# A two-block fp32 network on one core: tanh for sigmoid, powers on GpSimd for square roots, opened output products, regrouped layer A, and a scheduler that counts shared-port time

## Chip, core and metric

The kernel runs on one NeuronCore of a Trainium2 chip. The metric is the device time of one execution in microseconds (us). All inputs and outputs are fp32.

## The reference, cut to what matters

The program is one forward pass over 512 tokens of width 1024: a gated linear recurrence (layer A), sliding-window attention (layer B), a second block with windowed attention and grid attention, and an MLP. Every norm is a root mean square over the width.

```python
# layer A, R = 1536, in blocks of 96 for the two gates
u = rmsnorm(x) @ w_in; xb, gate = u[:R], u[R:]
xb = conv4(xb)
r, i = sigmoid(xb @ wr + br), sigmoid(xb @ wi + bi)
a = exp(-8 r softplus(-lam)); b = sqrt(1 - a*a) * (i * xb)
x = x + (scan(a, b) * silu(gate)) @ w_out
# keys and values of layer B from this x; layer B, 16 heads of 64, window 128, sinks
q, gate = split(rmsnorm(x) @ w_in); q = rmsnorm(q per head)
x = x + (attention(q, k, v, sinks) * silu(gate)) @ w_out
# block 2: windowed attention a, grid attention b, merged by sigmoid gates
q_a, k_a, v_a, q_b, k_b, v_b, g_a, g_b = split(rms_norm(x) @ w_in)
m = sigmoid(g_a + bg_a) * (y_a @ w_pa) + sigmoid(g_b + bg_b) * (y_b @ w_pb)
x = x + m @ w_out
x = x + square(relu(rms_norm(x) @ w_up)) @ w_down
return rms_norm(x)
```

## The kernel before

The activations stand transposed: 128 features on the partitions, 512 tokens along a row. Each fp32 product is made from three products of rounded halves: a value is split in a high half (a copy to type fp32r, helper `A` with `AF.Copy`, line 305, 309 or 314) and a low half (value minus high half, `TT`, line 329, or `STT`, line 343, on VectorE). `mm3` issues high·high, high·low and low·high, all 512 columns wide, through `MMS` (line 370). Weights are split in the same way, per piece of 1024 columns: `raw_task` loads a piece by DMA (line 400) into a slot of the pool FB, `hi_task` lets ScalarE, VectorE (first eight pieces) or GpSimd make the high half, and `lo_task` always has VectorE make the low half. FB has 38 slots of 512 columns and holds nearly every intermediate; PSUM has 8 banks.

Jobs are Python generators that yield operations. The class `Sched` runs them all, gives every operation a booked duration, and in each step emits the one that can start first and scores best; so the order on every engine is a plan, and on the chip each engine works through its own list in that order. An operation may have options on several engines, and then the one that is booked to end first is taken. The function `main` runs the TensorE jobs strictly in the order in which `add` and `then` list them.

- `gemm` makes one 128-feature output: for 8 k pieces it is 24 matmuls, and its results are taken from PSUM by an `evac` task. `gemm_open(w, ns, kcut, ...)` first runs the k pieces below `kcut` for all outputs of `ns`, and then the rest, so that TensorE has work on the early activations while the later ones are being made.
- Layer A (`layer_a`): 12 products `xb` (convolution, split, restacking by DMA), four jobs `rg_job` (30 matmuls each, for both gates of three feature groups), 12 products `ga` for the output gate. `rg_post` makes tanh, exp, square root and the scan (line 817) for the three; `ga_evac` waits for each third product and then does sigmoid, two products and the split of `y_a`. `a_w_out` opens three outputs over the first 9 of 12 pieces.
- Norms (`rstd_chain`): the sum of squares goes through a matmul with ones, ScalarE's square root, and VectorE's reciprocal (line 363) over 512 columns; only norm b goes by tokens, that is over 4 columns, and then back by a diagonal matrix and a second matmul with ones.
- Layer B (`layer_b`): `w_kv`, then 16 products `b_w_in` with the 16 attention units (`attn_unit`, four heads by one block of 128 tokens each) spread between them. A unit makes the masks (`PMUL`, line 357, GpSimd), score matmuls (256 wide), maxima (line 959, VectorE), exponentials (ScalarE), a division (GpSimd), transposes (line 394), and the products with v (256 wide). `q1_scale` makes the norms of q: square root on ScalarE, reciprocal and products on VectorE. `b_w_out` opens four outputs over 6 of 8 pieces; piece k needs `y1[k]`, which is whole when all four units of its group are.
- Block 2 (`block2`), the same in kind; its end is `w_pb` (opened), whose results `pb_evac` turns into `mrg`, and then `w_out_2`, 8 plain products over `mrg`. `mlp` follows, and `fin_stats`, `fin_task` and `fin_out` make the last norm and store it.

Sigmoid, square root and exp stand in three different tables of ScalarE (tanh stands with exp, and with sigmoid as well); `Sched` books a switch at 1283 ns and avoids it by a score.

Of the kernel before, what the change touches and what calls it, by code (L numbers as in the profile page):

```python
# [89 lines left out]
class Sched:  # L90
# [43 lines left out]
    def run(self):  # L134
        while self.tasks:
# [97 lines left out]
def kernel(ctx: ExitStack, tc: tile.TileContext, io: dict, out: bass.AP):  # L233
# [592 lines left out]
    def ga_evac(n, b):  # L826
        j = n - KR
        gat[j] = yield from scaled(b, n_a)
        if j % 3 == 2:
            sg = {}  # L830
            for i in range(j - 2, j + 1):
                sg[i] = yield from fa.get()
                yield A(f_(sg[i]), f_(gat[i]), AF.Sigmoid)
            for i in range(j - 2, j + 1):
                yield TT(f_(gat[i]), f_(gat[i]), f_(sg[i]), ALU.mult)
                fa.free(sg[i])
            for i in range(j - 2, j + 1):
                yield lambda: i in hs
# [1008 lines left out]
```

## Time and profile before

| | us |
|---|---|
| median of three runs | 1162.11 (1161.6 to 1163.76) |
| the profiled execution, device time | 1162.27 |
| its span, first to last instruction | 1160.4 |
| TensorE busy in it | 1129.6 (97%) |
| VectorE, ScalarE, GpSimd busy | 772.6, 419.4, 273.9 |

Busy time counts an engine as busy while one of its instructions is under way. The mean granted clock of TensorE over the span is 0.988 of 2.4 GHz. A table by stretches gives for each engine the busy time and, in brackets, the number of instructions; matmuls overlap, so their mean duration is longer than the distance from one to the next, and the rate is read from the chain of waits, which gives a length and a count.

### The profile page before, as it was taken

The page shows a single profiled execution, that of the slowest core. Times are in us where ns is not written, and L with a number is a line of the kernel's source. Part 1 is how long each engine was busy: PE and PEld are TensorE (multiplying, and loading weights), DVE is VectorE, ACT ScalarE, POOL GpSimd, SP SyncE. Part 2 cuts the span into 40 slices and gives each one's busy share as a digit, 9 for nine tenths or more (in the row PEclk, how much of TensorE's full clock was granted, in tenths as well). Part 3 has the DMA queues.
Part 4 walks back from the last instruction along what each step waited for, and adds up shares of the span by engine and source line. Part 5 has one row for each costly group of instructions (what it writes and reads, how often), then busy time and mean ns, then how long its engine had stood idle before and what let it go on. Part 6 is the DMA issues. An engine that isn't in the chain of part 4 may idle for free.

```text
span 1160.4 us, 14950 instructions
## 1 busy us (share of the span) xinstructions
PE 1129.6 (97%) x5444; PEld 943.4 (81%) x5444; DVE 772.6 (67%) x1362; ACT 419.4 (36%) x809; POOL 273.9 (24%) x356
## 2 busy tenths in 40 slices
PE   8999799999999899999999999899999999999997
PEld 5888588888888678888888888688888888888887
DVE  8999998756778888567666464867654224556332
ACT  5348841224887641166542225111111121111111
POOL 2111152023644633033223223312110002112000
PEclk9999899999999899999999999999999999999999
DMA  7252436207242330821371643432243322233001
GB/s 284 76 140 58 132 122 209 91 1 206 68 123 87 101 127 1 239 89 64 91 236 57 175 134 116 142 130 91 73 127 91 122 78 91 73 109 109 1 1 73
DMA packets 45641, 125.85 MB, mean 108 GB/s; under 512 B 6144, under 2 KB 8576, under 8 KB 45568
## 3 DMA queue, kind: packets, MB, share of 16 engines
q1 hardware_dynamic: 45568, 124.90, 34.3%
q8 instruction: 43, 0.70, 0.2%
q14 instruction: 30, 0.25, 0.1%
HBM read 104.95 MB, written 2.10 MB: 92 GB/s over the span
## 4 chain that ended last, share of the span: by engine, by line
PE 90%; DVE 6%; ACT 1%; DMA 1%; issue 1%; SPq 0%; DVEq 0%; ACTq 0%
PE ps L370 87%; PE ps L394 3%; DVE fb L329 2%; DVE rb L329 2%; DVE fb L817 1%; ACT rb L305 1%; DVE fb L959 0%; DMA rb<-rb 0%; DMA fb<-in_x 0%; ACT fb L305 0%; SPq L400 0%; DMA fb<-in_wg 0%; DVE fb L343 0%; DVE rb L309 0%; ACT L305 0%
## 5 line engine op out<-in xcount | busy, mean ns | idle before, releaser
L370 PE MATMUL ps<-rb 128*128 128x512 f32 (+2 forms) x5008 | 1095.5, 378 | 18.3 <-ACT rb L305 10.3
L370 PEld LDWEIGHTS ps<-rb 128*128 128x128 f32 x5008 | 895.0, 189 | 193.9 <-ACT rb L305 12.5
L329 DVE TENSOR_TENSOR rb<-fb,rb 128x1024 fp32r<-128x1024 f32 (+5 forms) x301 | 298.7, 1015 | 62.4 <-ACT rb L305 57.0
L314 POOL TENSOR_SCALAR rb<-fb 128x1024 fp32r<-128x1024 f32 (+5 forms) x154 | 173.7, 1137 | 677.9 <-PE ps L370 541.4
L305 ACT ACTIVATE rb<-fb 128x512 fp32r<-128x512 f32 (+5 forms) x127 | 94.6, 752 | 335.4 <-DVE fb L343 154.0
L329 DVE TENSOR_TENSOR fb<-ps,fb 128x512 f32<-128x512 f32 (+2 forms) x170 | 102.4, 604 | 154.8 <-PE ps L370 141.5
L329 DVE TENSOR_TENSOR fb<-fb 128x512 f32<-128x512 f32 (+1 forms) x140 | 99.8, 725 | 25.2 <-ACT rb L305 20.9
L357 POOL TENSOR_SCALAR fb<-fb,sm 128x256 f32<-128x256 f32 (+2 forms) x128 | 68.7, 556 | 152.0 <-DVE sm L363 105.3
L329 DVE TENSOR_TENSOR rb<-ps,rb 128x512 fp32r<-128x512 f32 (+1 forms) x92 | 58.1, 640 | 42.1 <-ACT rb L305 39.8
L305 ACT ACTIVATE rb<-ps 128x512 fp32r<-128x512 f32 (+1 forms) x92 | 50.5, 558 | 89.0 <-PE ps L394 66.4
L305 ACT ACTIVATE fb<-fb,sm 128x256 f32<-128x256 f32 (+2 forms) x128 | 65.3, 512 | 36.4 <-DVE sm L351 25.9
L305 ACT ACTIVATE rb<-fb,vec 128x512 fp32r<-128x512 f32 x41 | 28.5, 720 | 111.2 <-DVE fb L329 109.2
L343 DVE SCALAR_TENSOR_TENSOR fb<-ps,fb 128x512 f32<-128x512 f32 x36 | 24.9, 691 | 52.5 <-PE ps L370 52.4
L305 ACT ACT_TABLE_LOAD x44 | 56.5, 1283 | 7.9 <-DVE fb L736 4.3
L305 ACT ACTIVATE fb<-fb 128x512 f32<-128x512 f32 (+1 forms) x60 | 35.1, 610 | 62.6 <-DVE fb L329 60.8
L394 PE MATMUL ps<-ident,fb 128*128 128x128 f32 x328 | 48.3, 273 | 3.4 <-POOL fb L357 1.9
L394 PEld LDWEIGHTS ps<-ident,fb 128*128 128x128 f32 x328 | 39.2, 140 | 10.5 <-POOL fb L357 2.3
L305 ACT ACTIVATE fb<-ps 64x256 f32<-64x256 f32 (+1 forms) x57 | 23.6, 414 | 44.1 <-PE ps L370 34.5
L959 DVE CUSTOM_DVE_ANT_0 fb<-ps,fb 128x256 f32<-128x256 f32 (+1 forms) x64 | 28.5, 486 | 12.5 <-DMA fb<-in_mbe 5.2
L357 POOL TENSOR_SCALAR fb<-fb,sm_qs 128x256 f32<-128x256 f32 (+1 forms) x64 | 31.1, 509 | 10.5 <-DMA fb<-in_mk 10.5
L343 DVE SCALAR_TENSOR_TENSOR rb<-fb,vec,rb 128x512 fp32r<-128x512 f32 x41 | 31.3, 781 | 0.3 <-ACT rb L305 0.2
L959 DVE CUSTOM_DVE_ANT_0 fb<-ps,fb,sm_qt 128x256 f32<-128x256 f32 (+1 forms) x64 | 26.4, 440 | 4.8 <-PE ps L370 3.5
(71 smaller groups left out, 286.9 us busy)
## 6 DMA issues: line engine op xcount, KB each, us to landing
fb<-in_w_in SPq DMA_DIRECT2D x34, 512.0 KB, 3.8
rb<-rb SPq DMA_DIRECT2D x128, 128.0 KB, 3.0
fb<-in_w_up SPq DMA_DIRECT2D x32, 512.0 KB, 3.5
fb<-in_w_down SPq DMA_DIRECT2D x32, 512.0 KB, 3.6
fb<-in_a_w_in SPq DMA_DIRECT2D x22, 512.0 KB, 4.5
fb<-in_b_w_in SPq DMA_DIRECT2D x16, 512.0 KB, 4.5
fb<-in_a_w_out SPq DMA_DIRECT2D x8, 512.0 KB, 3.6
fb<-in_w_out SPq DMA_DIRECT2D x8, 512.0 KB, 3.7
```

The costliest lines, as they stand in the source:

```text
L305: opts = [("ACT", dur, lambda: nc.scalar.activation(out=o, in_=i, func=fn, **kw), TABLES.get(fn))]
L314: lambda: nc.gpsimd.tensor_scalar(out=o, in0=i, scalar1=1.0, scalar2=1.0, op0=ALU.mult, op1=ALU.mult), None,
L329: lambda: nc.vector.tensor_tensor(out=o, in0=a, in1=b, op=op), None,
L343: lambda: nc.vector.scalar_tensor_tensor(out=o, in0=a, scalar=s, in1=b, op0=op0, op1=op1), None,
L357: lambda: nc.gpsimd.tensor_scalar(out=o, in0=a, scalar1=s, scalar2=1.0, op0=ALU.mult, op1=ALU.mult), None,
L370: nc.tensor.matmul(out=o, lhsT=l, rhs=r, start=st, stop=sp)
L394: nc.tensor.transpose(o, i, ident)
L817: nc.vector.tensor_tensor_scan(out=f_(h), data0=f_(rg[0, j]), data1=f_(th[j]), initial=0.0, op0=ALU.mult, op1=ALU.add)
L959: nc.vector.tensor_tensor_reduce(out=pt[:, h, 0:nk], in0=PS[:, b, o0:o0 + nk], in1=m, scale=sc, scalar=-3.0e38, op0=ALU.add, op1=ALU.max, ...
```

## The change

1. Sigmoid becomes tanh of half the argument: `ga_evac`, `g1_evac` and `g2_evac` work on each product alone; the factors 0.5 and the `+1` go into products that were there (`STT` for `TT`). The gates r and i of layer A keep their sigmoid, and `rg_post` its square root.
2. Square roots with a reciprocal become a power of -0.5 on GpSimd (`GTT`, booked 350 ns + 165 ns a column). All norms go by tokens (4 columns), `q1_scale` does both halves at once on GpSimd (16 columns, five small operations behind each other), and the last norm uses it too (2 columns).
3. `layer_a` alternates its groups; `a_w_out` opens four outputs over 8 pieces. `w_kv`, the first three of `w_in_2`, the first three of `w_out_2` and of `w_up` are opened over 4 pieces; their first pieces of weights are half as wide.
4. `Sched` lengthens a VectorE or GpSimd operation that has no PSUM input by a share of its overlap with the other, and GpSimd is charged 600 ns more where another engine could do the work.

```diff
+AVOID = 600.0
+STRETCH = {"DVE": 0.3, "POOL": 0.6}
...
+    def _shared(self, eng, op, s, dur):
+        if any(k[0].startswith("ps") for k in op.r):
+            return dur
+        mine, other = (("DVE", "POOL"), ("POOL", "DVE"))[eng == "POOL"]
+        ov = sum(max(0.0, min(s + dur, e) - max(s, b)) for b, e in self.port[other])
+        self.clock[other] += ov * STRETCH[other]
+        dur += ov * STRETCH[mine]
...
-                        if best is None or s + o[1] < best[0]:
+                        f = s + o[1] + (AVOID if o[0] == "POOL" and len(t.op.opts) > 1 else 0.0)
+                        if best is None or f < best[0]:
...
+    def GTS(o, a, s1, s2):
+        return Op([("POOL", 420.0, ...
+    def GTT(o, a, b, op):
+        return Op([("POOL", 350.0 + 165.0 * _free(o) if op == ALU.pow else 200.0, ...
...
     def rstd_chain(nrm):
-        if not nrm.tokens:
-            yield MMS([(p_(b), ones, acc, True, True, 858.0)])
-            yield A(f_(bc), p_(b), AF.Sqrt, scale=1.0 / D, bias=eps)
-            yield RECIP(f_(bc), f_(bc))
...
-        yield A(std, PS[:, b, 0:4], AF.Sqrt, scale=1.0 / D, bias=eps)
-        yield RECIP(col, std)
+        yield TS(ms, PS[:, b, 0:4], 1.0 / D, ALU.mult, EPS, ALU.add)
+        yield GTT(col, ms, half[:, 0:4], ALU.pow)
...
     def ga_evac(n, b):
+        gat[j] = yield from scaled(b, n_a, 0.5)
+        yield A(f_(sg), f_(gat[j]), AF.Tanh)
+        yield STT(f_(gat[j]), f_(sg), 1.0, f_(gat[j]), ALU.add, ALU.mult)
+        yield lambda: j in hs
+        yield TT(f_(hs[j]), f_(hs[j]), f_(gat[j]), ALU.mult)
...
     def layer_a():
-        xb(2, 9)
+        xb(2, 6)
+        ga(0,1)
         rg_job(0)
+        xb(6, 9)
+        ga(1, 3)
+        rg_job(1)
         xb(9, 12)
-        rg_job(1)
-        ga(0, 2)
+        ga(3, 5)
         rg_job(2)
-        ga(2, 4)
+        ga(5, 7)
         rg_job(3)
-        ga(4, 12)
+        ga(7, 12)
-        gemm_open("a_w_out", [0, 1, 2], 9, KR, y_a, ev, 1)
+        gemm_open("a_w_out", [0, 1, 2, 3], 8, KR, y_a, ev, 1)
...
     def q1_scale(hg):
+        yield TT(v(t), v(PS[:, b, 0:16]), bc(c2), ALU.mult)
+        yield GTS(t, t, 1.0 / 64, EPS)
+        yield GTT(sd, t, half, ALU.pow)
+        yield GTT(t, t, sd, ALU.mult)
+        yield GTT(v(sd), v(sd), bc(n_b.col), ALU.mult)
+        yield GTT(v(t), v(t), bc(n_b.std), ALU.mult)
...
+        gemm_open("w_kv", [0, 1], 4, KD, act_kv, lambda n, b: (v1_evac if n else k1_evac)(n, b), 1)
+        gemm_open("w_in_2", list(first), 4, KD, act_m, lambda n, b: first[n](n, b), 1)
+        gemm_open("w_out_2", [0, 1, 2], 4, KD, mrg, ev, 1)
+        gemm_open("w_up", [0, 1, 2], 4, KD, act_f, up_evac)
...
     def fin_stats(th):
-            yield A(stdf[:, k:k + 1], PS[:, bs[k], 0:1], AF.Sqrt, scale=1.0 / D, bias=eps)
+            yield TS(stdf[:, k:k + 1], PS[:, bs[k], 0:1], 1.0 / D, ALU.mult, EPS, ALU.add)
-        yield RECIP(colf[:, c], stdf[:, c])
+        yield GTT(colf[:, c], stdf[:, c], half[:, 0:2], ALU.pow)
```

The plan changes on every engine. Three places follow, each as the engine's list reads before and in the changed kernel.

VectorE at the norm of layer A, before: the low halves of two weight pieces, the reciprocal, then the first products taken from PSUM.

```order
L329 TENSOR_TENSOR fb<-fb 128x512 x2
L329 TENSOR_TENSOR rb<-fb,rb 128x1024 x2
L363 RECIPROCAL fb<-fb 128x512
L343 SCALAR_TENSOR_TENSOR lt<-vec 128x12
L736 MEMSET fb 128x3 x4
L329 TENSOR_TENSOR rb<-fb,rb 128x1024
L329 TENSOR_TENSOR fb<-ps,fb 128x512 x4
```

VectorE at the same place, changed:

```order
L346 TENSOR_TENSOR fb<-fb 128x512 x2
L346 TENSOR_TENSOR rb<-fb,rb 128x1024 x2
L368 TENSOR_SCALAR sm<-ps 128x4
L346 TENSOR_TENSOR fb<-ident,col_a 128x512
L759 MEMSET fb 128x3 x3
L346 TENSOR_TENSOR fb<-ps,fb 128x512 x2
```

The reciprocal over 512 columns is gone; a 4-column step and the diagonal stand in its place, with the power on GpSimd between them.

ScalarE in the middle of layer B, before (`sm_qs` are the norms of q, `fb,sm<-fb,sm` the exponentials with their sums):

```order
L305 ACTIVATE fb,sm<-fb,sm 128x256 x4
L305 ACTIVATE sm<-sm 128x4
L305 ACT_TABLE_LOAD
L305 ACTIVATE sm_qs_0_2373<-sm_qt_0_2372,eps 128x8
L305 ACT_TABLE_LOAD
L305 ACTIVATE fb,sm<-fb,sm 128x256 x2
L305 ACTIVATE rb<-ps 128x512
```

ScalarE there, changed:

```order
L322 ACT_TABLE_LOAD
L322 ACTIVATE fb,sm<-fb,sm 128x128 x4
L322 ACTIVATE sm<-sm 128x4
L322 ACTIVATE fb,sm<-fb,sm 128x256 x2
L322 ACTIVATE rb<-fb 128x1024
L322 ACTIVATE fb,sm<-fb,sm 128x256 x3
L322 ACTIVATE sm<-sm 128x4
L322 ACTIVATE fb,sm<-fb,sm 128x256 x3
```

The load shown last is the last one of the whole list: 45 loads become 18, of which 16 are at the start and in layer A in the changed kernel and 15 before.

TensorE at the end of `b_w_in`, before; the first row holds its last three matmuls, the 512-wide ones behind it are `b_w_out`, the 256-wide ones scores or products with v, and `ident` marks transposes:

```order
L370 MATMUL ps<-rb 128x512 x6
L370 MATMUL ps<-rb 128x256 x22
L370 MATMUL ps<-rb 128x512 x3
L370 MATMUL ps<-rb 128x256 x8
L394 MATMUL ps<-ident,fb 128x128 x4
L370 MATMUL ps<-rb 128x512 x6
L394 MATMUL ps<-ident,fb 128x128 x8
L370 MATMUL ps<-rb 128x256 x8
L394 MATMUL ps<-ident,fb 128x128 x4
L370 MATMUL ps<-rb 128x256 x16
```

TensorE there, changed; again the first row holds the last three of `b_w_in`:

```order
L396 MATMUL ps<-rb 128x512 x15
L420 MATMUL ps<-ident,fb 128x128 x4
L396 MATMUL ps<-rb 128x512 x9
L396 MATMUL ps<-rb 128x256 x4
L396 MATMUL ps<-rb 128x512 x18
L420 MATMUL ps<-ident,fb 128x128 x4
L396 MATMUL ps<-rb 128x512 x6
L420 MATMUL ps<-ident,fb 128x128 x8
L396 MATMUL ps<-rb 128x512 x3
L396 MATMUL ps<-rb 128x256 x2
```

Behind the last matmul of `b_w_in` layer B has 82 matmuls of 256 columns and 40 transposes left before, and 28 and 28 in the changed list: there all scores are done by then, and the last four units have only their transposes and products with v to come.

## Rows read from the trace of the kernel before

**Rows 1.** The page's part 1: busy us, share of the span, instructions.

```profile
PE 1129.6 (97%) x5444; PEld 943.4 (81%) x5444; DVE 772.6 (67%) x1362; ACT 419.4 (36%) x809; POOL 273.9 (24%) x356
```

**Rows 2.** Stretches: length, busy (count) of PE, PEld, DVE, ACT, POOL, then PEclk.

```profile
118.00:134.00 16.00, 7.62 (x21) 5.36 (x20) 15.81 (x24) 14.17 (x20) 0.00 (x0) 0.68 0.41 125
...
384.00:426.00 42.00, 35.18 (x185) 28.39 (x184) 34.37 (x89) 23.16 (x67) 20.93 (x36) 0.92 0.38 128
...
742.00:758.00 16.00, 12.07 (x41) 8.67 (x40) 14.07 (x19) 3.77 (x6) 2.97 (x2) 0.79 0.57 188
758.00:1140.00 382.00, 382.00 (x1746) 318.39 (x1745) 190.18 (x225) 55.87 (x72) 46.12 (x42) 1.00 0.26 81
```

**Rows 3.** Chain of waits, 740 to 1160: start, length, what.

```profile
754.38 370.53 PE ps L370 x1624
1124.91 0.87 PE ps L394 x8
...
1127.29 6.48 PE ps L370 x54
```

**Rows 4.** Groups on PE by shape, 384 to 426: count, busy us, mean ns, idle before.

```profile
L370 PE MATMUL ps<-rb 128*128 128x512 f32 x74 | 22.4, 438 | 3.1 <-ACT rb L305 1.7 <-DVE rb L329 1.3
L370 PE MATMUL ps<-rb 128*128 128x256 f32 x67 | 11.1, 299 | 1.2 <-DVE rb L329 1.2
L394 PE MATMUL ps<-ident,fb 128*128 128x128 f32 x44 | 6.6, 278 | 2.5 <-POOL fb L357 1.9 <-DVE sm L959 0.6
```

**Rows 5.** Timeline 121 to 128.5: start us, us, instruction, idle before and releaser.

```profile
121.84 1.23 DVE L817 TENSOR_TENSOR_SCAN fb<-fb 128x512 f32<-128x512 f32 x1
...
123.13 3.88 SPq L400 DMA_DIRECT2D fb<-in_wg  x2
...
126.17 0.84 ACT L305 ACTIVATE rb<-fb 128x768 fp32r<-128x768 f32 x1 [0.92 <-DMA fb<-in_wg]
...
127.07 1.91 PE L370 MATMUL ps<-rb 128*128 128x512 f32 x3 [8.38 <-ACT rb L305]
```

**Rows 6.** Groups by shape, whole span: count, busy us, mean ns, idle before.

```profile
L329 DVE TENSOR_TENSOR rb<-fb,rb 128x512 fp32r<-128x512 f32 x101 | 74.5, 749 | 2.4 <-ACT rb L305 0.9
...
L363 DVE RECIPROCAL fb<-fb 128x512 f32<-128x512 f32 x4 | 13.4, 3344 | 1.5 <-ACT fb L305 1.5
...
L370 PE MATMUL ps<-ones,fb 128*128 128x1 f32 x24 | 3.1, 237 | 0.0
L314 POOL TENSOR_SCALAR rb<-fb 128x128 fp32r<-128x128 f32 x7 | 2.9, 422 | 5.5 <-PE ps L370 5.5
...
L351 DVE TENSOR_SCALAR sm<-sm 128x4 f32<-128x4 f32 x8 | 1.9, 238 | 0.1
L329 DVE TENSOR_TENSOR fb<-ident,col_b 128x512 f32<-128x512 f32 x1 | 0.7, 692 | 0.0
```

**Rows 7.** Timelines of VectorE, 22 to 35 and 193 to 205.

```profile
32.90 2.47 DVE L329 TENSOR_TENSOR fb<-ps,fb 128x512 f32<-128x512 f32 x4
...
193.10 4.03 DVE L329 TENSOR_TENSOR rb<-fb,rb 128x512 fp32r<-128x512 f32 x5
201.15 0.69 DVE L329 TENSOR_TENSOR fb<-ps,fb 128x512 f32<-128x512 f32 x1 [4.02 <-PE ps L370]
```

**Rows 8.** Groups on ScalarE by shape, 250 to 400.

```profile
L305 ACT ACT_TABLE_LOAD x20 | 25.7, 1283 | 0.4
```

**Rows 9.** Timeline 380 to 427: a table load on ScalarE and what follows it.

```profile
389.93 1.28 ACT L305 ACT_TABLE_LOAD   x1
...
391.22 0.40 ACT L305 ACTIVATE fb<-fb,sm 128x128 f32<-128x128 f32 x1
```

**Rows 10.** A stretch of layer B, columns as in Rows 2.

```profile
280.00:400.00 120.00, 114.75 (x666) 99.36 (x664) 94.23 (x307) 91.15 (x222) 64.34 (x124) 1.00 0.35 108
```

**Rows 11.** The chain's last steps: start, length, what.

```profile
1154.01 0.49 ACT std_o L305 x2
...
1154.53 0.18 DVE col_o L363
```

More of the change, by code (lines that the diff above doesn't have):

```diff
@@ L183, in run @@
             else:
-                end = s + dur
+                end = s + (self._shared(eng, t.op, s, dur) if eng in self.port else dur)
                 self.clock[eng] = end
@@ L360, in PMUL @@
         )], [a, s], [o])
+    def GTS(o, a, s1, s2):
+        return Op([(
+            "POOL", 420.0,
+            lambda: nc.gpsimd.tensor_scalar(out=o, in0=a, scalar1=s1, scalar2=s2, op0=ALU.mult, op1=ALU.add), None,
+        )], [a], [o])
+    def GTT(o, a, b, op):
+        return Op([("POOL", 350.0 + 165.0 * _free(o) if op == ALU.pow else 200.0, lambda: nc.gpsimd.tensor_tensor(out=o, in0=a, in1=b, op=op), None)], [a, b], [o])
     def RECIP(o, a):
@@ L827, in ga_evac @@
         j = n - KR
[L828 to L838, printed above, removed]
-                yield TT(f_(hs[i]), f_(hs[i]), f_(gat[i]), ALU.mult)
-                fa.free(gat[i])
-                s = yield from split(f_(hs[i]))
-                fa.free(hs[i])
-                put(y_a, i, s)
+        gat[j] = yield from scaled(b, n_a, 0.5)
+        sg = yield from fa.get()
+        yield A(f_(sg), f_(gat[j]), AF.Tanh)
+        yield STT(f_(gat[j]), f_(sg), 1.0, f_(gat[j]), ALU.add, ALU.mult)
+        fa.free(sg)
+        yield lambda: j in hs
+        yield TT(f_(hs[j]), f_(hs[j]), f_(gat[j]), ALU.mult)
+        fa.free(gat[j])
+        s = yield from split(f_(hs[j]))
+        fa.free(hs[j])
+        put(y_a, j, s)
     n_b = norm("b", True)
@@ L1043 @@
     sg1 = {}
-    g1 = {}
     y1raw = {}
@@ L1454, in pb_evac @@
         g = f_(gts[8 + j])
-        yield TT(g, p_(b), g, ALU.mult)
+        yield STT(g, g, 1.0, p_(b), ALU.add, ALU.mult)
         pa.free(b)
@@ L1458, in pb_evac @@
         fa.free(gts[j])
-        s = yield from split(g)
+        s = yield from split(g, 0.5)
         fa.free(gts[8 + j])
@@ L1468, in z @@
             gemm("w_in_2", n, KD, act_m, evac, prio=prio)
-        z(4, k2_evac, 1)
-        z(5, v2_evac, 1)
-        for j in range(4):
+        first = {4: k2_evac, 5: v2_evac, 0: qa_evac}
+        gemm_open("w_in_2", list(first), 4, KD, act_m, lambda n, b: first[n](n, b), 1)
+        for j in range(1, 4):
             z(j, qa_evac, 1)
@@ L1520, in block2 @@
         ev = x_update([("mlp_g", act_f)], n_f)
-        for j in range(KD):
+        gemm_open("w_out_2", [0, 1, 2], 4, KD, mrg, ev, 1)
+        for j in range(3, KD):
             gemm("w_out_2", j, KD, mrg, ev, prio=1)
@@ L1637, in mlp @@
         H = NFF // 2
-        for j in range(H):
+        gemm_open("w_up", [0, 1, 2], 4, KD, act_f, up_evac)
+        for j in range(3, H):
             gemm("w_up", j, KD, act_f, up_evac)
@@ L1696 @@
         nc.vector.memset(eps, EPS)
-        nc.scalar.activation(out=lt[:, 0, 0:1], in_=eps, func=AF.Sqrt)
+        nc.vector.memset(half, -0.5)
+        nc.scalar.activation(out=lt[:, 0, 0:1], in_=eps, func=AF.Exp)
+        S.table = "exp"
         for j in range(WARM):
```

82 lines of the change are left out of this document (38 added, 44 removed).

## The prediction

> **What bounds it now.** TensorE is busy for 1129.6 of 1160.4 us [rows 1]. What it does hardly changes, so the change can only win back time in which TensorE is not at its full rate. I read that rate first, from the chain of waits: 370.53 us for 1624 matmuls of 512 columns is 0.228 us each, 6.48 us for 54 of 256 columns is 0.120 us, and 0.87 us for 8 transposes is 0.109 us [rows 3]. Then I read the busy time by stretches: the last long one, 758 to 1140, is full, 382 of 382 us at a granted clock of 1.00 [rows 2]. Three stretches are not. To see what each loses, I price its matmuls at full rate:
>
> - Stretch A, 118 to 134 (the middle of layer A): 21 matmuls x 0.228 = 4.8 us of work in 16 us [rows 2], so 11.2 us are lost.
> - Stretch B, 384 to 426 (the end of layer B): 74 x 0.228 + 67 x 0.120 + 44 x 0.109 = 16.9 + 8.0 + 4.8 = 29.7 us of work in 42 us [rows 2, 4], so 12.3 us are lost.
> - Stretch D, 742 to 758 (from `w_pb` to `w_out_2`): 41 x 0.228 = 9.3 us in 16 us [rows 2], so 6.7 us are lost.
>
> Together that is 30.2 us. Only part of it is idle time: the granted clock averages 0.68, 0.92 and 0.79 there [rows 2], so behind each idle time TensorE ran for a while at the 1.2 GHz level, and a stall that goes takes that loss with it. Outside these stretches the start-up (some 25 us, in which x and the first weights arrive) and the tail remain; they are no target of the change.
>
> **Stretch A, about -10.2 us.** TensorE waits 8.38 us for one weight piece of the gates: its DMA is issued at 123.13, just when the scan that began at 121.84 ends and a slot of FB comes free; the copy ends at 127.0 and TensorE restarts [rows 5]. VectorE is busy for 15.81 of the 16 us [rows 2], so the cause is VectorE's backlog, which keeps slots occupied. A gate job is what fills it: for each of three features a scan of 1.23 us [rows 5] and four products or squares of 0.7 to 0.8 us, which with two weight pieces is 14 to 15 us of VectorE against 30 x 0.228 = 6.8 us of TensorE. An output-gate product is the cure: some 4.2 us of VectorE against 24 x 0.228 = 5.5 us. Before, three gate jobs come with two output-gate products between them; now there are five, 16.4 us more work for TensorE before it asks for the third job's weights. I went through both lists of VectorE and priced each instruction by the mean of its group by shape: in the changed list every weight piece of layer A's front is ready before TensorE asks for it, by 2.4 us at the tightest, while the list of before comes out late exactly at the third gate job. The next limit is the crossing into `a_w_out`. From the first product out of PSUM, 32.90, to the last low half of `y_a`, the first of the five at 193.10 [rows 7], so done at 193.8, VectorE needs 160.9 us for a list priced at 167.0. The changed list is priced at 168.6, which is 162.4 at the same pace. It begins earlier, though not by the whole 3.34 us of the reciprocal [rows 6], since VectorE waits for the power and for the second matmul with ones: about 30.8, which gives 193.2. TensorE ended the first `a_w_out` product just before 201.15 [rows 7]; 11.2 us earlier, with an opening 15 matmuls longer (96 for 81, 3.4 us) and the last three still to go (0.7), it asks for the last piece at 201.1 - 11.2 + 3.4 - 0.7 = 192.6, with the longer norm about 193. So the two are level; I leave 1 us of waits, between 0 and 6.
>
> **Stretch B, about -8.3 us.** Here the products of `b_w_in`, which cover the attention units, are used up, and TensorE lives on what units deliver: its gaps end on low halves (VectorE), on divided probabilities (GpSimd) and on copies (ScalarE) [rows 4]. The list after that point shrinks from 82 matmuls of 256 columns and 40 transposes to 28 and 28, since the plan runs the units earlier; it can, because ScalarE loses the 20 table loads, 25.7 us, that lie between 250 and 400 [rows 8], out of 91.15 us of its busy time between 280 and 400 [rows 10]. The last four units still need, on ScalarE, some 2.4 us of exponentials each, then division, transposes, split, products with v and the gate, while `b_w_out` has 72 matmuls, 16.4 us, that need no piece of the last group. I take 4 us lost where 12.3 were, with 1 and 10 as ends. The load that stood in this chain takes 1.28 us, and the next exponential starts 0.01 us behind its end [rows 9]. The Trainium skill (ScalarE: Activation LUTs, What ACT_TABLE_LOAD costs) adds about 1.38 us of drain to each switch; this trace does not show it, and by the page the sum would be 1.4 us lower.
>
> **Stretch D, about -5.7 us.** TensorE gets to piece 4 of `mrg` after 12 matmuls, 2.7 us, and VectorE is late with it. Opening three outputs over 4 pieces puts 36 matmuls, 8.2 us, ahead of it: 5.5 us more cover for 3.9 us of waits (the idle part of 16 - 12.07 [rows 2]). VectorE's work per piece keeps its number of operations; sigmoid is no part of it. I leave 1 us, between 0 and 4, for the early pieces, which are now asked for faster.
>
> **What is added.** Three norms (a, m, f) get four 1-column matmuls more: 12 x 3.1/24 = +1.6 us [rows 6]. The powers have no row. Below, a GpSimd instruction takes 0.42 us even when small; above, the slowest elementwise kind in the trace is the reciprocal with 3.34 us [rows 6]. The code books 1.0 us for 4 columns and 3.0 for 16, nearer the lower end, and I take that. In the norms 15 to 18 matmuls, 3.4 to 4.1 us, stand between the two matmuls with ones and cover 0.24 + 1.0 + 0.69 us of chain [rows 6]; at 3.34 us each norm would wait up to 0.9 us, 3.6 in all. In the tail nothing covers: two square roots, 0.49 us, and a reciprocal, 0.18 [rows 11], become two VectorE steps and a power, about +0.6, between +0.2 and +3. The four chains of `q1_scale` put some 20 us on GpSimd in layer B, which has 120 - 64.3 = 55.7 us free between 280 and 400 [rows 10]; the cover is `b_w_in`. The opened `w_kv`, `w_in_2` and `w_up` meet no stall before, so I count them at nothing; their cover is the dense TensorE itself, and their half pieces put eight more DMAs on SP, which the span has room for. The 600 ns charge moves next to nothing: ScalarE's 1024-wide copies go from 42 to 44. For new short waits in the reordered lists I add 1 us, between 0 and 5.
>
> **Sum.** Against the profiled execution: 1162.3 - 10.2 - 8.3 - 5.7 + 1.6 + 0.6 + 1.0 = 1141.3 us. That execution is 0.2 us over the median of 1162.11, so I say 1141.
>
> **Rivals.**
>
> *The stalls move rather than go.* VectorE's work in layer A stays at 168.6 for 167.0 us, and it works its list in order. If waits for ScalarE, which keeps its table loads there, cost it 5 us in the new order, `y_a` comes 5 us after TensorE asks; with the lower clock behind such a wait some 8 us of A return, and the time is 1149. For it: VectorE is the full engine in A. Against it: in B and D the cover is plainly longer.
>
> *Slower: the powers clog GpSimd.* If a column of the power costs c, the four 16-column chains cost 4 x (16c + 2.1) us on GpSimd in layer B, where 55.7 us are free [rows 10]; above c = 0.74 us every unit's division waits in that queue, and TensorE behind it. The norms then wait 4 x (4c - 2.6) more. Both together eat the 21 us of gain at about c = 1.0, six times the booked value; at 1.1 the time is about 1172. For it: no row prices the power, and the smallest GpSimd instruction already takes 0.42 us against 0.18 for the reciprocal it replaces in the tail [rows 6, 11]. The Trainium skill (GPSIMD Engine Reference, Engine selection) sends elementwise work to VectorE, GpSimd being about half as fast with two inputs; no row here has such an operation on GpSimd, and by that factor the powers would be cheap and this rival void.
>
> *No effect.* If the three stalls are set by lengths of chains and not by order or cover, each returns whole at the next dependency: 1162. Against it: stretch A's wait is a slot that comes late, and more cover is there in all three.
>
> **Chances.** Forecast (1134 to 1147) 0.64; the stalls move (1147 to 1155) 0.21; even better than 1134, 0.04; no effect 0.04; slower 0.07. A measurement of this kernel tells 0.2%, 2.3 us, from no change, so faster is 0.89, the same 0.04, slower 0.07. The range runs from A, B and D at their low ends with no new waits (-1 - 3 - 1 - 1) and a point less for the tail, 1134, to the second case with some of the added terms at their upper ends, 1154.
>
> **What would show it.** Right: no wait of TensorE over 2 us between 100 and 190, granted clock 1.00 there; at the end of layer B fewer than 6 us lost by the same count; no table load after 300; the step into `w_out_2` with under 2 us of waits; a GpSimd power of about 1 us. Wrong: a wait for a low half at the start of `a_w_out`, waits of TensorE for GpSimd in layer B, a power of several us, or a new half-clock stretch somewhere else.

## The result, and the profile after

The changed kernel takes 1150.86 us (median of four runs, 1149.55 to 1151.42); the kernel before took 1162.93 beside it. The ratio is 0.9893, 95% interval 0.9874 to 0.9912. So it is faster by 12 us (1.1%). That is inside the stated range of 1134 to 1154, but little more than half of the 21 us that were forecast: the time does not lie in the forecast's own case (1134 to 1147) but in that of its first rival (1147 to 1155).

To see where, I priced every matmul at full rate (0.227 us for 512 columns, 0.120 for 256, 0.109 for a transpose, after the rates of [rows 3]; 0.175 for 384 and 0.112 for one, the usual distance from start to start) and took the rest of the distance to the next matmul's start as lost: TensorE is idle then, or runs at the lower clock. Summed by place in the profiled executions, one of each kernel, in us (executions of the same list differ by 1 to 3 us at a place, as the last section shows):

| place | before | after | difference | predicted |
|---|---|---|---|---|
| matmuls at full rate | 1108.9 | 1111.6 | +2.7 | +1.6 (norms) |
| start, 0 to 30 | 9.0 | 7.4 | -1.6 | not counted |
| A: 40 to 60 and 100 to 180 | 11.6 | 2.3 | -9.3 | -10.2 |
| B: 280 to 430 | 13.1 | 8.1 | -5.0 | -8.3 |
| D: 725 to 765 | 7.1 | 5.6 | -1.5 | -5.7 |
| 465 to 580 | 0.5 | 2.0 | +1.5 | in the +1.0 |
| 630 to 665 | 1.2 | 1.7 | +0.5 | in the +1.0 |
| elsewhere, with the tail | 10.9 | 10.9 | 0.0 | +0.6 |
| device time | 1162.27 | 1149.55 | -12.7 | -21.0 |

Part 1 of the page after, to be read against [rows 1]: TensorE's busy time falls by 2.7 us only, ScalarE's by 33.5, GpSimd's rises by 22.2.

```profile
PE 1126.9 (98%) x5468; PEld 942.2 (82%) x5468; DVE 758.6 (66%) x1335; ACT 385.9 (34%) x782; POOL 296.1 (26%) x392
```

Stretches of the kernel after (length, then busy us and count of PE, PEld, DVE, ACT, POOL, then PEclk), for A, B, D and a place that was full before:

```profile
118.00:134.00 16.00, 16.00 (x73) 13.23 (x71) 16.00 (x21) 11.64 (x17) 3.88 (x3) 1.00 0.29 90
366.00:412.00 46.00, 41.99 (x221) 34.54 (x221) 39.12 (x99) 23.18 (x67) 20.97 (x34) 0.96 0.44 144
728.00:748.00 20.00, 16.54 (x66) 12.44 (x65) 15.47 (x23) 4.42 (x7) 6.15 (x6) 0.91 0.72 235
44.00:56.00 12.00, 10.38 (x45) 7.98 (x44) 12.00 (x19) 7.09 (x10) 1.04 (x2) 1.00 0.56 158
```

A is full at clock 1.00, where [rows 2] had 7.62 of 16 us at 0.68. B and D have shrunk, but are still there, and part of what shrank is the clock: the granted clock was at 1.2 of 2.4 GHz for 6.8 us in each of them before (399.5 to 406.4 and 751.1 to 757.9), and for 3.4 us after (408.8 to 412.2 and 739.9 to 743.3). The last row is new: gate job 0 now stands one product, 5.5 us, behind the sixth `xb`, where it stood behind the ninth, and TensorE waits for the DMAs that restack its input, as its timeline there shows:

```profile
43.65 5.60 PE L396 MATMUL ps<-rb 128*128 128x512 f32 x24
49.48 1.39 PE L396 MATMUL ps<-rb 128*128 128x512 f32 x5 [0.23 <-DMA rb<-rb]
52.26 0.96 PE L396 MATMUL ps<-rb 128*128 128x512 f32 x3 [1.38 <-DMA rb<-rb]
```

At D, TensorE's waits for low halves sum to nearly the same in both kernels, as the view of waits shows, before (735 to 760) and after (715 to 770), each with total, number and longest:

```profile
PE ps L370 <- DVE rb L329: 3.9, 3, 2.3
PE ps L396 <- DVE rb L360: 3.5, 3, 2.2
```

The three after are for low halves of `mrg` (line 360), the first for the second piece:

```profile
737.65 0.98 PE L396 MATMUL ps<-rb 128*128 128x512 f32 x3 [2.16 <-DVE rb L360]
739.45 1.33 PE L396 MATMUL ps<-rb 128*128 128x512 f32 x3 [0.83 <-DVE rb L360]
741.26 1.22 PE L396 MATMUL ps<-rb 128*128 128x512 f32 x2 [0.47 <-DVE rb L360]
```

VectorE's timeline just before says why. It makes sums of later pieces (`fb<-fb`) first, and the low half that TensorE waits for, `rb<-fb,rb` at 736.91, after them; two of the sums take 1.13 and 1.07 us instead of 0.68:

```profile
733.67 0.67 DVE L360 SCALAR_TENSOR_TENSOR fb<-fb,ps 128x512 f32<-128x512 f32 x1
734.27 1.13 DVE L346 TENSOR_TENSOR fb<-fb 128x512 f32<-128x512 f32 x1
735.32 0.67 DVE L360 SCALAR_TENSOR_TENSOR fb<-fb,ps 128x512 f32<-128x512 f32 x1
735.92 1.07 DVE L346 TENSOR_TENSOR fb<-fb 128x512 f32<-128x512 f32 x1
736.91 0.68 DVE L360 SCALAR_TENSOR_TENSOR rb<-fb,rb 128x512 fp32r<-128x512 f32 x1
```

Under the two long ones GpSimd copied weights, one piece of 1024 columns and two of 512:

```profile
733.81 1.05 POOL L331 TENSOR_SCALAR rb<-fb 128x1024 fp32r<-128x1024 f32 x1 [2.41 <-DVE fb L346]
734.82 1.05 POOL L331 TENSOR_SCALAR rb<-fb 128x512 fp32r<-128x512 f32 x1
735.84 0.61 POOL L331 TENSOR_SCALAR rb<-fb 128x512 fp32r<-128x512 f32 x1
```

The Trainium skill (SBUF — State Buffer, Who interferes with whom) says that a VectorE operation with two SBUF inputs contends with a GpSimd instruction that reads SBUF, and one with at most one SBUF input, outside its two-port modes, does not. The five rows agree: the products with one input in PSUM keep 0.67 us. The same section of the Trainium skill calls the shared port pair an exclusive lock, and the rows agree with that as well, for the two engines take turns: the first long sum ends at 735.40, 0.54 us behind the copy that ended at 734.86; the next copy ends some 0.5 us behind that sum and lasts 1.05 us, where one of its size that meets nothing takes some 0.62; and the second long sum ends 0.54 us behind the copy that ended at 736.45. It is so in the whole run: all 33 `TENSOR_TENSOR` of VectorE over 512 columns with no input in PSUM that last more than 0.72 us end 0.53 to 0.54 us behind the end of a GpSimd instruction.

The last wait of B has such stretched operations too: at 406 the split of the last two pieces of `y1` runs under three GpSimd copies. The CAST takes 1.15 us instead of 0.43, and the two low halves of 512 columns 1.08 and 1.09 us instead of 0.68 (the third in the row has 1024 columns and takes its usual 1.21). TensorE waits 1.57 us for the first of them.

```profile
405.56 3.13 POOL L331 TENSOR_SCALAR rb<-fb 128x1024 fp32r<-128x1024 f32 x3 [4.05 <-PE ps L396]
406.06 1.15 DVE L326 CAST rb<-fb 128x512 fp32r<-128x512 f32 x1
407.13 3.23 DVE L346 TENSOR_TENSOR rb<-fb,rb 128x512 fp32r<-128x512 f32 x3
408.27 2.24 PE L396 MATMUL ps<-rb 128*128 128x512 f32 x5 [1.57 <-DVE rb L346]
```

The powers, and what they replaced, by groups over the whole span (count, busy us, mean ns):

```profile
L386 POOL TENSOR_TENSOR sm_qs<-sm_qt,half 128x16 f32<-128x16 f32 x4 | 11.6, 2912 | 0.2
L386 POOL TENSOR_TENSOR col_o<-std_o,half 128x2 f32<-128x2 f32 x2 | 1.4, 704 | 38.8 <-DVE std_o L368 38.8
L386 POOL TENSOR_TENSOR col_m<-sm,half 128x4 f32<-128x4 f32 x1 | 1.0, 1017 | 9.0 <-DVE sm L368 9.0
L396 PE MATMUL ps<-ones,fb 128*128 128x1 f32 x48 | 5.8, 236 | 0.0
L322 ACT ACT_TABLE_LOAD x17 | 21.8, 1283 | 2.0 <-issue 1.3 <-DVE fb L360 0.4
```

### The profile page after: what moved, and what is told of

It is laid out like the page before. It is cut to its first block, busy times and chain, and to the rows that moved or that the text cites. A ratio compares the mean times of both kernels' runs of the same rounds, so it can differ in the third digit from the quotient of the medians.

```text
span 1147.7 us, 14995 instructions
## 1 busy us (share of the span) xinstructions
PE 1126.9 (98%) x5468; PEld 942.2 (82%) x5468; DVE 758.6 (66%) x1335; ACT 385.9 (34%) x782; POOL 296.1 (26%) x392
## 4 chain that ended last, share of the span: by engine, by line
PE 87%; DVE 5%; DMA 2%; issue 2%; POOL 1%; ACT 1%; SPq 0%; POOLq 0%; DVEq 0%; ACTq 0%
PE ps L396 85%; PE ps L420 3%; DVE fb L360 2%; DVE rb L346 2%; DVE fb L346 1%; POOL fb L374 1%; DMA fb<-in_mk 1%; DMA rb<-rb 1%; DVE fb L980 0%; DMA fb<-in_w_out 0%; DVE rb L360 0%; ACT rb L322 0%; DMA fb<-in_x 0%; ACT fb L322 0%; SPq L426 0%
## 5 line engine op out<-in xcount | busy, mean ns | idle before, releaser
L396 PE MATMUL ps<-rb 128*128 128x512 f32 (+1 forms) x5008 | 1093.1, 377 | 11.8 <-DVE rb L360 3.7
L331 POOL TENSOR_SCALAR rb<-fb 128x1024 fp32r<-128x1024 f32 (+4 forms) x159 | 169.3, 1076 | 605.7 <-PE ps L396 465.5
L346 DVE TENSOR_TENSOR rb<-fb,rb 128x512 fp32r<-128x512 f32 (+5 forms) x301 | 285.9, 974 | 47.7 <-ACT rb L322 39.7
L322 ACT ACTIVATE rb<-fb 128x512 fp32r<-128x512 f32 (+4 forms) x134 | 99.0, 747 | 305.0 <-DVE fb L360 155.6
L346 DVE TENSOR_TENSOR fb<-ps,fb 128x512 f32<-128x512 f32 (+2 forms) x134 | 78.1, 584 | 155.4 <-PE ps L396 143.7
L346 DVE TENSOR_TENSOR fb<-fb 128x512 f32<-128x512 f32 (+1 forms) x120 | 89.7, 754 | 22.9 <-ACT rb L322 20.8
L360 DVE SCALAR_TENSOR_TENSOR fb<-ps,fb 128x512 f32<-128x512 f32 x56 | 38.5, 687 | 59.2 <-PE ps L396 59.1
L374 POOL TENSOR_SCALAR fb<-fb,sm_qt 128x256 f32<-128x256 f32 (+1 forms) x64 | 33.3, 546 | 2.2 <-DMA fb<-in_mk 2.1
L360 DVE SCALAR_TENSOR_TENSOR fb<-fb,vec 128x512 f32<-128x512 f32 x36 | 30.8, 872 | 0.0
L980 DVE CUSTOM_DVE_ANT_0 fb<-ps,fb,sm_qs 128x256 f32<-128x256 f32 (+1 forms) x64 | 26.7, 444 | 5.7 <-PE ps L396 3.3
```

Source lines behind the costliest of these rows:

```text
L322: opts = [("ACT", dur, lambda: nc.scalar.activation(out=o, in_=i, func=fn, **kw), TABLES.get(fn))]
L331: lambda: nc.gpsimd.tensor_scalar(out=o, in0=i, scalar1=1.0, scalar2=1.0, op0=ALU.mult, op1=ALU.mult), None,
L346: lambda: nc.vector.tensor_tensor(out=o, in0=a, in1=b, op=op), None,
L360: lambda: nc.vector.scalar_tensor_tensor(out=o, in0=a, scalar=s, in1=b, op0=op0, op1=op1), None,
L374: lambda: nc.gpsimd.tensor_scalar(out=o, in0=a, scalar1=s, scalar2=1.0, op0=ALU.mult, op1=ALU.mult), None,
L396: nc.tensor.matmul(out=o, lhsT=l, rhs=r, start=st, stop=sp)
```

## The experiments

All times are medians; "lost" is counted as in the table above. The changed kernel stands at 1150.9.

**e1: the old order of layer A in the changed kernel.**

```diff
-        xb(2, 6)
-        ga(0,1)
+        xb(2, 9)
         rg_job(0)
-        xb(6, 9)
-        ga(1, 3)
+        xb(9, 12)
         rg_job(1)
...
-        gemm_open("a_w_out", [0, 1, 2, 3], 8, KR, y_a, ev, 1)
+        gemm_open("a_w_out", [0, 1, 2], 9, KR, y_a, ev, 1)
```

> The changed kernel, with layer A's order of the kernel before put back (three more xb products ahead of the first gate job, no output-gate product between the first two, a_w_out opened for three outputs over nine pieces). Theory 1 (stretch A's loss is the order's: three gate jobs too close together for VectorE): the wait for the third gate job's weights at 118 to 134 comes back and the time rises by about 9.5 us, to 1160, between 1157 and 1163. Theory 2 (the gain in layer A comes from what layer A's chains no longer do: no 512-wide reciprocal, tanh without a table load, each output-gate product finished on its own): without the order the stretch stays full and the time is 1151, between 1149 and 1153.

Measured: 1167.20 (1165.26 to 1167.77). Stretch A loses 12.3 us again, none of it at 40 to 60, through the very wait of [rows 5]:

```profile
128.84 0.80 PE L396 MATMUL ps<-rb 128*128 128x512 f32 x1 [9.99 <-ACT rb L322]
```

Locally that is theory 1: 12.3 against 2.3 is 10.0 us for the order. But the time rose by 16.3, beyond theory 1's range, since the plan behind is made anew: 465 to 580 loses 5.4 (2.0), B 9.5 (8.1), D 6.8 (5.6), the start 8.2 (7.4).

**e2: the new order in the kernel before.** The edit of e1 the other way round, on the kernel before:

```diff
-        xb(2, 9)
+        xb(2, 6)
+        ga(0,1)
         rg_job(0)
...
```

> The kernel before, with only the changed order of layer A and the changed opening of a_w_out; sigmoid, square roots, norms, scheduler and all else stay. Theory 1 (the order alone fills stretch A): 1163 less 9.5 is 1153.5, between 1151 and 1156, and no lost time at 118 to 134. Theory 2 (the order needs the other parts): over 1159. With both theories in part true (output-gate products are finished three at a time here, so their sigmoids come late and hold slots of FB): between 1156 and 1159.

Measured: 1168.02 (1164.10 to 1170.64), 0.4% slower than before (ratio 1.0040, 1.0025 to 1.0055). Again theory 1 holds in the place, where the stretch is full but for 0.9 us:

```profile
100.00:180.00 80.00, 79.29 (x350) 65.38 (x349) 79.93 (x102) 52.20 (x75) 24.34 (x18) 1.00 0.35 114
```

A loses 4.1 (with 3.2 for the restacking DMAs) instead of 11.6. But 280 to 430 loses 17.1 (13.1), 465 to 580 3.8 (0.5), D 8.2 (7.1) and the start 10.1 (9.0). So the time is theory 2's, over 1159: the order alone wins its place and loses as much or more elsewhere, and it gains nothing without the other parts.

**e3: w_out_2 not opened.**

```diff
-        gemm_open("w_out_2", [0, 1, 2], 4, KD, mrg, ev, 1)
-        for j in range(3, KD):
+        for j in range(KD):
             gemm("w_out_2", j, KD, mrg, ev, prio=1)
```

> The changed kernel with w_out_2 as eight plain products again, not opened; nothing else. Theory 1 (the opening hides the first pieces, but VectorE's list makes the second low half of mrg late, so that the opening gained only the 1.5 us seen): 1152.4, between 1151.5 and 1153.5. Theory 2 (as predicted, the opening is worth 5.7 us, and something else in the new list takes 4 us back): 1156.5, between 1155 and 1158. Theory 3 (VectorE's list alone sets when w_out_2 ends its first outputs, opened or not): 1151, within 1 us.

Measured: 1153.59 (1149.87 to 1154.88); ratio to before 0.9916 (0.9903 to 0.9928), which overlaps that of the changed kernel. D loses 7.3 us against 5.6. That favours theory 1, just above its range: in this list the opening is worth 1.7 us, not 5.7.

**e4: the norms of q back on ScalarE and VectorE.** `q1_scale` as in the kernel before; 30 table loads for 18.

```diff
-        yield GTT(sd, t, half, ALU.pow)
...
+            yield A(sd, t, AF.Sqrt, scale=1.0 / 64, bias=eps)
+            yield RECIP(t, sd)
...
```

> The changed kernel with q1_scale as before: square root on ScalarE, reciprocal and products on VectorE, and so 12 more table loads of 1.28 us, all in layer B (30 in all for 18). Theory 1 (the table loads kept the attention units late, and the drain of layer B was long for that): the loss at 366 to 426 grows from 7.4 to about 11 or 12 us, and the time is 1155, between 1153 and 1157. Theory 2 (ScalarE has slack in layer B, and the units run earlier for the sigmoids that have gone or for another order alone): 1151, between 1149.5 and 1152.5.

Measured: 1165.94 (1163.82 to 1168.49). 280 to 430 loses 22.9 us (8.1), with ScalarE's copies as the last releaser, in TensorE's waits at 375 to 430:

```profile
PE ps L396 <- ACT rb L322: 8.5, 2, 5.3
PE ps L396 <- DVE rb L346: 1.9, 3, 0.9
```

The direction is theory 1's, the size more than three times it. The plan was made anew here too, so e9 tries the loads alone.

**e5: mrg first.**

```diff
-        gemm_open("w_pb", [0, 1, 2, 3], 3, 4, yb, pb_evac)
+        gemm_open("w_pb", [0, 1, 2, 3], 3, 4, yb, pb_evac, -1)
         for j in range(4, KD):
-            gemm("w_pb", j, 4, yb, pb_evac, prio=1)
+            gemm("w_pb", j, 4, yb, pb_evac, prio=-1)
```

> The changed kernel with pb_evac at priority -1 in all eight products; the plan is the same row by row up to the last products of pa_evac, and then VectorE makes the low half of each piece of mrg before the products of later pieces and before low halves of weights. Theory 1 (the opening was long enough, and VectorE's list had the second low half of mrg too far back): the waits at 735 to 742 go from 4.6 us of lost time to under 1.5, and the time is 1147, between 1145.5 and 1148.5. Theory 2 (the sum of VectorE's work between w_pb and w_out_2 is too much whatever its order): the wait moves to a later piece or to low halves of weights, and the time stays at 1151, within 1 us.

Measured: 1145.27 (1144.30 to 1148.23); ratio to before 0.9857 (0.9844 to 0.9870). D loses 0.7 us instead of 5.6. TensorE's list is the same, and VectorE's is the same up to 722. TensorE does not stop there, at full clock, though VectorE is now busy for the whole stretch:

```profile
728.00:748.00 20.00, 20.00 (x90) 16.43 (x88) 20.00 (x27) 4.43 (x7) 10.99 (x8) 1.00 0.59 200
```

Theory 1. It even copes with two-input operations over 512 columns that GpSimd stretches to 0.93 to 1.52 us.

**e6: w_out_2's copies on ScalarE.**

```diff
-   also="copy" if i < 8 else "pool",
+   also="copy" if i < 8 else None if plan[i].name in ('in_w_out_2',) else "pool",
```

> The changed kernel with the high halves of w_out_2's weights on ScalarE alone instead of GpSimd; the plan is the same up to w_pb. Theory 1 (GpSimd's copies stretch VectorE's operations in this stretch, 0.68 to 1.13 and 1.07 us for those under a copy, and this makes mrg late): VectorE's products and low halves at 728 to 742 all take 0.65 to 0.70 us, the loss there falls from 5.6 to about 3, and the time is 1148.5, between 1147 and 1150. Theory 2 (the order of VectorE's list makes mrg late and sharing costs under 1 us): 1150 to 1151, with the same wait for the second low half of mrg.

Measured: 1146.85 (1145.74 to 1148.66), ratio 0.9868 (0.9855 to 0.9881). D loses 1.6 us, and VectorE's operations at 728 to 742 are all at their short time:

```profile
L360 DVE SCALAR_TENSOR_TENSOR rb<-fb,rb 128x512 fp32r<-128x512 f32 x8 | 5.2, 686 | 0.0
L346 DVE TENSOR_TENSOR fb<-fb 128x512 f32<-128x512 f32 x5 | 3.4, 686 | 0.0
```

The gain is larger than theory 1's (a loss of about 3, and 1147 to 1150), and the plan had also moved `mrg`'s low halves forward; so e12 keeps the list.

**e7: b_w_out's copies on ScalarE.**

```diff
-   also="copy" if i < 8 else "pool",
+   also="copy" if i < 8 else None if plan[i].name in ('in_b_w_out',) else "pool",
```

> The changed kernel with the high halves of b_w_out's weights on ScalarE alone; the plan is the same up to the last products of b_w_in. Theory 1 (GpSimd's copies at 405 to 409 stretch the split of the last two pieces of y1, CAST 1.15 us and low halves 1.1 instead of 0.7, and that makes the wait of 1.57 us there): the loss at 400 to 412 falls from 4.3 to about 2.5, and the time is 1149, between 1147.5 and 1150. Theory 2 (ScalarE's copies now stand ahead of exponentials of the last units): the loss at 366 to 412 grows, and the time is 1152, between 1151 and 1154.

Measured: 1155.40 (1150.99 to 1160.19). In the place the split of the last `y1` runs at its short times again (CAST 0.43, low halves of 512 columns 0.68 us; the third in the row has 1024), and 360 to 430 loses 5.7 (7.5):

```profile
408.51 0.43 DVE L326 CAST rb<-fb 128x512 fp32r<-128x512 f32 x1
408.85 2.42 DVE L346 TENSOR_TENSOR rb<-fb,rb 128x512 fp32r<-128x512 f32 x3
```

But most of these 1.8 us are not the split's. e3 and e6 have the changed kernel's lists on all engines up to 700 us, stretched split and waits of 0.49 and 1.57 us included, and lose 6.2 and 6.3 us at 360 to 430. In both the granted clock did not fall there; in the changed kernel it was at 1.2 GHz from 408.8 to 412.2. The stretch 404 to 414 in the changed kernel and in e3, and e3's wait (columns as above, and timeline):

```profile
404.00:414.00 10.00, 7.94 (x27) 5.57 (x26) 8.66 (x11) 2.05 (x4) 4.37 (x5) 0.83 0.17 58
404.00:414.00 10.00, 7.88 (x33) 5.66 (x32) 9.42 (x13) 2.64 (x5) 5.01 (x5) 1.00 0.19 66
408.85 5.39 PE L396 MATMUL ps<-rb 128*128 128x512 f32 x21 [1.57 <-DVE rb L346]
```

So against these two e7 wins some 0.5 us in the place, with a new wait of 1.86 us for a copy on ScalarE, and theory 1's 1.8 us are not shown. In a plan made anew, 465 to 580 loses 5.5 (2.0) and D 7.6 (5.6), and the time is above the range of either theory.

**e8: the scheduler part off.**

```diff
-AVOID = 600.0
-STRETCH = {"DVE": 0.3, "POOL": 0.6}
+AVOID = 0.0
+STRETCH = {"DVE": 0.0, "POOL": 0.0}
```

> The changed kernel with the scheduler's two new numbers at zero: AVOID 0, so that GpSimd is charged nothing more, and STRETCH 0, so that overlap lengthens nothing in the booking. Every other part stays. Theory 1 (the scheduler part moves next to nothing, as predicted; 111 instead of 102 copies of 1024 columns go to GpSimd): layer A keeps no loss, the time is within 2 us of 1151. Theory 2 (the plan is only good because overlaps are booked): losses of 2 us and more at places that are full now, such as 300 to 320 and 490 to 530, and a time of 1156 to 1163.

Measured: 1152.70 (1151.42 to 1153.54). Theory 1. 280 to 430 loses 8.7 (8.1), D 5.7 (5.6), A 3.4 (2.3).

**e9: table loads back, the list kept.** In eight of sixteen units of layer B:

```diff
+        def emit():
+            if twice:
+                nc.scalar.activation(out=junk, in_=eps, func=AF.Sqrt)
+            nc.scalar.activation(out=o, in_=i, func=fn, **kw)
```

> The changed kernel with its plan unchanged row by row, but eight of the sixteen units of layer B issue a square root of one unused column before the exponential of their sinks, which makes two table loads each: 16 loads more, 20.5 us of ScalarE, about as many as the kernel before had between 250 and 400 (20 loads, 25.7 us). Theory 1 (the loads themselves keep the units late, so their removal gave stretch B its 5 us): the loss at 366 to 426 grows from 7.4 to 11 to 14 us, and the time is 1156, between 1154 and 1160. Theory 2 (ScalarE has room for the loads, and stretch B got shorter because the plan could be made in another order): the loss there stays within 2 us of 7.4 and the time within 2.5 us of 1151.

Measured: 1157.10 (1153.92 to 1159.69). The time is theory 1's, the place only in part: the profiled execution (1153.92, the fastest) loses 11.8 us at 280 to 430 instead of 8.1, with 3.4 us at the lower clock in both, and nothing much elsewhere. The loads alone are worth 3.7 us in the place and 6.2 by the medians, not the 15 of e4.

**e10: mrg first, and gate job 0 one product later.** On e5:

```diff
         xb(2, 6)
+        xb(6, 7)
         ga(0,1)
         rg_job(0)
-        xb(6, 9)
+        xb(7, 9)
```

> The kernel of e5_mrg_first with one more xb product before the first output-gate product and the first gate job (7 and 1 ahead of it, not 6 and 1). Theory 1 (the new wait at 48 to 52 is for the restacking DMAs of the first three xb, which come 5.5 us too early before the gate job): the 2.2 us lost there go, the rest stays as in e5, and the time is 1143, between 1141.5 and 1145. Theory 2 (the plan behind it is made anew, and the losses elsewhere move by several us as in e1, e2 and e4): the loss at 48 to 52 goes, but the time is 1146 or more.

Measured: 1145.55 (1142.60 to 1147.75), ratio 0.9855 (0.9838 to 0.9872), level with e5. The loss at 40 to 60 is gone, and a wait for restacking comes back at a later gate job, as TensorE's waits at 40 to 240 show:

```profile
PE ps L396 <- DMA rb<-rb: 1.9, 1, 1.9
```

A loses 2.1 us there; the median lies between the two theories.

**e11: mrg and y1 first.** On e5:

```diff
-                    S.spawn(y1_gate(q[i], s + i), 1.5)
+                    S.spawn(y1_gate(q[i], s + i), -1)
```

> The kernel of e5_mrg_first with y1_gate at priority -1 instead of 1.5, so that the pieces of y1 go before low halves of weights and before other units on VectorE. Theory 1 (what held for mrg holds for y1: its low halves stand too far back in VectorE's list): the loss at 366 to 412 falls from 7.4 to about 4, and the time is 1142, between 1140 and 1144. Theory 2 (the last units of layer B set that loss by the length of their chains, not by the place of y1 in the list): the loss there stays at 6 us or more, and the time is 1144.5 or above.

Measured: 1149.51 (1148.47 to 1150.10): theory 2, and worse. 360 to 430 loses 10.4 (7.5 in the changed kernel), now behind the divisions on GpSimd (waits at 366 to 412):

```profile
PE ps L420 <- POOL fb L374: 5.7, 5, 2.1
```

**e12: w_out_2's copies on ScalarE, all lists kept.** In the option that was booked on GpSimd:

```diff
-   lambda: nc.gpsimd.tensor_scalar(out=o, in0=i, ...
+   lambda: nc.scalar.activation(out=o, in_=i, func=fn) if act else nc.gpsimd.tensor_scalar(
```

> The changed kernel with every list kept row by row, VectorE's among them, except that the copies of w_out_2's weights that GpSimd made are made by ScalarE at the same place of the plan. It parts the two things that e6 changed together. Theory 1 (the order of VectorE's list makes mrg late, sharing with GpSimd only adds): VectorE's operations at 728 to 742 take 0.65 to 0.70 us, which brings the second low half of mrg forward by the 0.9 us that the two stretched operations lost, the loss falls from 5.6 to about 4.5, and the time is 1150, between 1149 and 1151. Theory 2 (sharing is what makes mrg late): the loss falls to under 2 us, and the time is 1147, between 1145.5 and 1148.5. Theory 3 (the weight copies wait behind mrg's own copies on ScalarE): new waits for ScalarE or later weight halves, and 1151 or more.

Measured: 1151.78 (1147.71 to 1153.69). D loses 4.7 us against 5.6, the theory's 4.5, but not for the theory's reason. TensorE's three waits there are as long as in the changed kernel (3.9 us against 3.5); what is less is time at the lower clock, 3.4 us of it at D in the changed kernel and none in this execution:

```profile
PE ps L397 <- DVE rb L361: 3.9, 3, 2.2
740.80 0.96 PE L397 MATMUL ps<-rb 128*128 128x512 f32 x3 [2.21 <-DVE rb L361]
```

Theory 3 shows as well: VectorE twice waits 0.62 us for a copy, here the second time, and the median is its 1151 or more. One sum, at 739.07, still takes 1.08 us under GpSimd's copies of `w_up`.

```profile
732.34 0.69 DVE L347 TENSOR_TENSOR rb<-fb,rb 128x512 fp32r<-128x512 f32 x1 [0.62 <-ACT rb L331]
```

So with this order of VectorE's list `mrg` is late even where the copies of `w_out_2` are off GpSimd, and e5, which changes that order alone, ends it. What sharing with GpSimd alone adds is not shown, since the new waits for ScalarE may have taken back what it cost.

## Why the prediction was right, and where not

The range held, the forecast's own number did not. The measured time lies in the band of the rival that the stalls move (0.21, against 0.64 for the forecast), but its mechanism, `y_a` late by waits for ScalarE in layer A, did not come: A is full. Two signs of being right failed, at the end of layer B (7.5 us lost, under 6 asked) and at the step into `w_out_2` (waits of 3.5 us, under 2 asked). That the rival's 1149 comes near is chance: B and D kept more of their losses than I took, and A did not.

- **A (-10.2; measured -9.3): right in cause and size.** The 90 us from 100 to 190 are full at clock 1.00, and no wait for a low half came at `a_w_out`. e1 and e2 show from both sides that the order does it. The 2.1 us at 40 to 60 were not foreseen: I costed SP's restacking DMAs nowhere.
- **B (-8.3; measured -5.0): the mechanism in part, the remainder mis-sized.** No table load came after 300, and e9 shows that loads in the units' chains cost about 4 us in the place. (Behind `b_w_in` 44 transposes stood before, as [rows 4] have it, not 40; the argument is the same.) But "I take 4 us lost where 12.3 were" was 7.5 in 360 to 430 and 0.6 before it. I had counted the exponentials and the cover of `b_w_out`, and neither the short waits on the way nor the clock behind them. Of the 7.5 us, 1.2 to 1.3 come and go with the clock in executions of the same list (e3, e6), and some 0.5 are what e7 wins against these two by taking the split out from under GpSimd's copies. What the other short waits, at 370 to 386, would need stays open. e4 lost 15 us with fewer loads than e9; how much of the rest is VectorE's small steps and how much the new plan was not parted.
- **D (-5.7; measured -1.5): the step that failed.** It was "I leave 1 us ... for the early pieces, which are now asked for faster". The cover for piece 4 was there, 36 matmuls, but I did not look in VectorE's changed list for where pieces 1 to 3 are finished: after sums and products of later pieces. So the waits only went from 3.9 to 3.5 us and now stand at these pieces; the 1.5 us won there are mainly 3.4 us less at the lower clock. e5 changes only that order and wins the missing 4.9 us, clock included; in e12, with the order kept and the copies of `w_out_2` off GpSimd, the waits stay.
- **Norms (+1.6; measured +2.7).** 24 more records of one column at 0.112 us. A 1-column fp32 matmul is two records in the trace, and I priced 12 instructions by the mean per record.
- **Powers: right.** 1.02 us for 4 columns and 2.91 for 16, with 1.0 and 3.0 taken. The rival that they clog GpSimd is void, since TensorE has no wait for GpSimd at 280 to 430. The tail is level.
- **The start (not counted; measured -1.6).** Executions of the same list as the changed kernel's differ by 1 us there. One wait of TensorE went, and it was not for the 3.34 us reciprocal, which begins later, at 28.44, but for VectorE's last sum of squares. Before, VectorE's operations took turns there with GpSimd's copies from 20.33 on (sums of 1.53 and 1.20 us for 0.69); in the changed list GpSimd is idle there until 25.95. The wait before:

```profile
25.76 1.10 PE L370 MATMUL ps<-fb,ones 128*128 128x512 f32 x2 [1.70 <-DVE fb L329]
```

- **New waits (+1.0; measured +2.0 at 465 to 665).** The opened `w_in_2`, counted at nothing, is followed at 478 by maxima that wait for the masks' DMA, and TensorE waits 0.8 us for them. In e3, with the same lists there, it does not wait at all, and 465 to 580 loses 0.7; so most of this is a spread between executions. Whether the opening has a part in it was not tried.
- **The scheduler part, counted at next to nothing:** e8, 1.8 us slower without it, agrees within the spread.

## What to carry to other kernels

An opened product only covers a late piece if the earlier pieces are finished in the order in which they will be read: look in the changed list of the engine that makes them, not only at the number of matmuls ahead. Where a planner orders everything, judge an ablation by the lost time at its own place and keep the list fixed where you can (e9, e12): e1, e2, e4 and e7 also moved the time by several us at places that they did not edit. And part lost time into waits and lower clock before putting a difference of 1 or 2 us down to an edit: in e7 and e12 it was the clock. The best kernels here are e5 and e10, 1.4% faster than before, and e5 is one priority away from the change.

## What the runs showed of the hardware that was not expected

Where a VectorE operation with two SBUF inputs meets a weight copy on GpSimd, the two do not run side by side at a lower rate, but take turns: each of the 33 stretched ones ends 0.53 to 0.54 us behind the end of a GpSimd instruction (the rows at D).

The granted clock is not a matter of the list alone. Behind the same wait of 1.57 us near 408 it was at 1.2 GHz for 3.4 us in the changed kernel (408.8 to 412.2), in e5 and in e12, and stayed at 2.4 GHz in e3 and e6, with the same lists up to there.

The same list does not wait the same everywhere either: VectorE's wait for the masks near 478 was 4.88 us in the changed kernel, 6.88 in e5 and 3.38 in e3, with the same instructions up to there, and TensorE stood still for 0.8, 2.8 and 0 us by it. In the changed kernel:

```profile
478.98 0.42 DVE L980 CUSTOM_DVE_ANT_0 fb<-ps,fb 128x256 f32<-128x256 f32 x1 [4.88 <-DMA fb<-in_mk]
```

And in e5:

```profile
481.87 0.42 DVE L980 CUSTOM_DVE_ANT_0 fb<-ps,fb 128x256 f32<-128x256 f32 x1 [6.88 <-DMA fb<-in_mk]
```

The DMA of 768 KB that ends these waits landed 7.7, 9.7 and 6.4 us behind its issue. That is a spread of 3.3 us that no edit made. Its reason is open: at 470 to 480 the DMA engines are 95%, 85% and 90% busy in the three.
